# Residual stream with tokens on partitions, and its products 512 columns at a time

## The chip, the cores and the metric

The kernel runs on one core of a Trainium2 chip. The metric is the device time of one execution in microseconds (us); three runs of the kernel before are compared by their median.

## What is computed

A decoder trunk of two layers over 256 tokens of 2048 features, all in float32. The reference, cut to its frame:

```python
for layer in range(DEPTH):                       # DEPTH = 2
    if layer < N_A:                              # layer 0
        h = h + mlstm_mixer(rms_norm(h, a_norm[layer]), ...)
    else:                                        # layer 1
        k_sh, v_sh = shared_kv(h, kv_norm, w_kv, positions)
        h = h + diff_attention(rms_norm(h, b_norm[j]), k_sh, v_sh, ...)
    h = h + conv_ffn(rms_norm(h, f_norm[layer]), w_up[layer], conv_w[layer], conv_b[layer], w_down[layer])
return rms_norm(h, final_norm)
```

The mixer projects the normed stream to q and k (1024 columns each), v and an output gate o (2048 each) and 16 gate columns, runs a gated linear attention of 8 heads, multiplies by sigmoid(o) and projects with `w_out` (2048 x 2048). The attention has `w_q` (2048 columns), `w_kv` (2048 for k, 2048 for v) and `w_o`. The feed-forward has `w_up` (2048 x 11264), a convolution over three tokens, a gate, and `w_down` (5632 x 2048).

## The kernel before

**Products of halves.** Each float32 operand is split into two halves that TensorE multiplies at full rate (type fp32r): h is the rounded value, l what is left. A product is wh xh + wh xl + wl xh. The activations' halves lie side by side in one block, `xh | xl`, of 128 features by 256 tokens each.

**`gemm` (L374)** takes 256 columns of a weight matrix at a time, a "pair" of 128 columns each, and walks over the k-tiles of 128 rows. `granule` (L353) brings weights: a DMA on SyncE's queue loads 8 k-tiles (1 MB) into one of five `raw` buffers, and four k-tiles at a time ScalarE (ACT) copies the h half (L369) and VectorE (DVE) subtracts the l half (L371) into one of five `w` buffers. In the usual, "wide" form two matmuls serve a k-tile and 128 columns: the stationary wh against the 512 moving columns `xh | xl`, and wl against the 256 of xh (L411). The two halves of the PSUM bank are added up at the end: ACT copies one out (L417) and DVE adds it (L418). Pairs listed in `narrow` use three matmuls of 256 moving columns, without that addition. With `tokens_out` the activations are stationary and the weights move; the form is the same. `gemm_by_tokens` (L422) does the last 256 columns of all, the first 128 tokens ahead of the others.

In what follows a unit is one k-tile times 128 stationary columns times 256 moving ones, in its three partial products: two matmuls wide, three narrow.

**The residual stream** (`hT`, 16 tiles of 128 features by 256 tokens) has features on partitions, as the products' operands do. `residual` (L441) adds a product to it; a `Norm` (L188) then makes the next operands from the same tile (`operand`, L207: one ACT and one DVE instruction) and sums squares over features on GpSimd (POOL, L204). `rstd` (L232) gets the row sums with tiny matmuls (`sums`, L250) and spreads 1/sqrt over the partitions.

**Beginning and end.** `x` comes in two k-tiles at a time between weight loads of two k-tiles and 256 columns (`x_in`, L455), is transposed by TensorE into `x_ps` (L464), and feeds the first pair of q; the q pairs follow one another, with the 16 gate columns (`gps`, L492) among them. At the end the last product's columns are scaled, transposed back to tokens on partitions (`out_ps`, L863; `rest_ps`, L871), and scaled by the norm in `tokens_done` (L878), which writes four DMAs of 512 columns for each half of the tokens.

**What sets the order.** The code emits small work "later", a number of granules behind a product (`later`, `tick`), and the framework's scheduler then reorders the instructions of each engine by a simulated timeline. Each engine runs its list in order. Weights, `x` and the output go through SyncE's one queue.

Of the kernel before, what the change touches and what calls it, by code (L numbers as in the profile page):

```python
# [19 lines left out]
P = 128  # L20
D = 2048
# [15 lines left out]
KC = 8  # L37
HC = 4
RAW = 5
FIRST = [0, 2, 4, 6, 8, 10, 12, 14]  # L40
HL = 5
WARM = 28
HT_DVE = (0, 1, 2, 4, 6)
CW = 256

# 500000 ** (-i / 16) in float32, once for each half of a rotary pair
# [19 lines left out]
def trunk(  # L66
# [11 lines left out]
    big = ctx.enter_context(tc.tile_pool(name="big", bufs=38))  # L78
# [17 lines left out]
    waiting, clock, splits, loads = [], [0, 0], [], []  # L96
# [11 lines left out]
    # the tensor engine's clock rises with use: have it up when the first operands come  # L108
# [14 lines left out]
    # mask_a: row q, column k, NEG where k > q; mask_s: row s, column t, NEG where s > t; each twice  # L123
# [10 lines left out]
    def columns(sources, name):  # L134
        """rows of 128 parameters each, transposed: column j has parameters 128 j .. 128 j + 127"""
# [40 lines left out]
    def parameters():  # L176
# [3 lines left out]
        # w_hnorm / 2: the sigmoid of the output gate is (1 + tanh) / 2  # L180
# [4 lines left out]
    stream = resid.tile([P, KD, T], F32, name="stream")  # L185
    hT = [stream[:, i] for i in range(KD)]

    class Norm:  # L188
        """Sum of squares over the features, and the operands (h * gain) split in two exact halves."""

        def __init__(self, gain_cols, name):
            self.cols, self.name = gain_cols, name
            self.r = self.rt = self.parts = None
            self.sets = [[None] * KD for _ in gain_cols]
            self.acc = work.tile([P, T], F32, tag="acc", name=f"acc_{name}")
            self.n = 0

        def squares(self, i):
            if self.n == 0:
                act.activation(self.acc, hT[i], AF.Square)  # L200
            else:
                sq = tmp("sq")
                act.activation(sq, hT[i], AF.Square)
                pool.tensor_tensor(self.acc, self.acc, sq, op=ALU.add)  # L204
            self.n += 1

        def operand(self, n, i):  # L207
            cols, at = self.cols[n]
            g = cols[:, at + i:at + i + 1]
            h, l, hl = block(F32R, f"x_{self.name}_{i}")  # L210
            act.activation(h, hT[i], AF.Identity, scale=g)
            dve.scalar_tensor_tensor(l, hT[i], g, h.bitcast(F32), op0=ALU.mult, op1=ALU.subtract)
            self.sets[n][i] = (h, l, hl)

        def add(self, i):
            self.operand(0, i)
            self.squares(i)

        def first(self, i, ps):
            """the same from the transposed input"""  # L220
            cols, at = self.cols[0]
            g = cols[:, at + i:at + i + 1]
            h, l, hl = block(F32R, f"x_{self.name}_{i}")
            act.activation(h, ps, AF.Identity, scale=g)
            dve.scalar_tensor_tensor(l, ps, g, h.bitcast(F32), op0=ALU.mult, op1=ALU.subtract)
            self.sets[0][i] = (h, l, hl)
            if i % 8 in HT_DVE:
                dve.tensor_copy(hT[i], ps)
            else:
                act.activation(hT[i], ps, AF.Copy)  # L230

        def rstd(self):  # L232
            """1 / sqrt(mean square + eps): rt per token on partitions, a column for each half of the tokens; r on every partition"""
            with tc.high_priority():
                v = work.tile([P, 2], F32, tag="v2", name="v2")
                if self.parts is None:
                    dve.tensor_scalar(v, sums(self.acc)[:, :2], 1.0 / D, EPS, op0=ALU.mult, op1=ALU.add)
                else:
                    dve.tensor_tensor(v, self.parts[:, 0], self.parts[:, 1], op=ALU.add)
                    dve.tensor_scalar(v, v, 1.0 / D, EPS, op0=ALU.mult, op1=ALU.add)  # L240
                self.rt = rsqrt(v, "rt", dve if self.parts is None else pool)
            self.spread() if self.parts is not None else later(1, self.spread)
# [7 lines left out]
    def sums(a):  # L250
        """the sums of a over the partitions: (P, 2), tokens on partitions, a column for each half of them"""
        ps = small_ps("sum_ps")
        for t in range(2):
            pe.matmul(ps[:, t:t + 1], a[:, t * P:(t + 1) * P], ones[:, 0:1], start=True, stop=True)
        return ps
# [20 lines left out]
    def spread(y):  # L276
        """(P, 2) with tokens on partitions to (P, T) with the same T tokens on every partition"""
# [39 lines left out]
    def weighted(v, p):  # L317
        """sum over s of p[s, t] v[s, :], a bank with t on partitions for each half of t"""
# [11 lines left out]
    def squares(banks):  # L330
        """the sum of squares of a head's 256 features, (P, 2)"""
# [5 lines left out]
    def normed_rows(banks, y):  # L337
        rows = []
        for t, ps in enumerate(banks):
            rows.append(tmp("nrm"))  # L340
# [3 lines left out]
    def turn(rows, name):  # L344
        """two (128 t, 256) to features on partitions, (2, T)"""
# [7 lines left out]
    def granule(w, c0, k0, kn, raws, j, hc=None, first=False, own=True):  # L353
        """the two halves of up to HC k-tiles of 256 columns; a load brings KC of them, at the very beginning HC"""
        at, hc = k0 % KC, hc or min(HC, kn - k0)
        if at == 0:
            raws[j] = wpool.tile([P, KC, CW], F32, tag="raw", name="raw", bufs=RAW)
        part = raws[j][:, at:at + hc]
        if first or at == 0:
            n = hc if first else min(KC, kn - k0)  # L360
            loads.append(nc.sync.dma_start(raws[j][:, at:at + n], w[k0 * P:(k0 + n) * P, c0:c0 + CW].rearrange("(k p) n -> p k n", p=P)))  # L361
        if not own:
# [4 lines left out]
            return pairs, None  # L367
# [566 lines left out]
```

## Time and profile before

| what | value |
|---|---|
| median of 3 runs | 2281.06 us (2280.37 to 2281.28) |
| profiled execution, first to last instruction | 2280.0 us |
| PE busy | 2267.8 us (99%) |
| DVE, ACT, POOL busy | 70%, 55%, 8% |
| HBM read | 413.86 MB, 182 GB/s over the span |

The profiled execution has one time, its span of 2280.0 us; the median of the timed runs is 1.1 us more, so differences are made against the span and added to the median. Times of a row are microseconds from the span's start, means are ns. A matmul's end is modelled in this profile, so the busy time of one (393 ns for 512 columns) is longer than its share of a steady stream; how many start in a stretch says what one costs.

### The profile page before, as it was taken

To read this page: it belongs to the slowest core of one execution; us is meant where nothing else is said; L and a number is where in the kernel's file an instruction comes from. 1 tells how busy PE (TensorE), PEld (TensorE's weight loads), DVE (VectorE), ACT (ScalarE), POOL (GpSimd) and SP (SyncE) were. 2 spreads that over 40 slices of the span, in tenths; PEclk is the share of its full clock that TensorE was granted. 3 is DMA by queue.
4 is the path that set the end of the run, shared out by engine and by line. 5 is a ranking of instruction groups with operands and counts; after the bars stand their busy time and mean duration, and the time that the engine had idled before them with its cause. 6 is when DMAs were issued, how large, how long until landed. Compare 5 with 4: busy or idle time off the path is not lost.

```text
span 2280.0 us, 34236 instructions
## 1 busy us (share of the span) xinstructions
PE 2267.8 (99%) x13318; PEld 1995.3 (88%) x13318; DVE 1588.7 (70%) x2667; ACT 1258.4 (55%) x2019; POOL 175.7 (8%) x379
## 2 busy tenths in 40 slices
PE   9999999999999999999999999999999999999998
PEld 8888888888888888888988888988888888888887
DVE  7756667777764677775588875677777556777755
ACT  6466555655554455655554556556555445555544
POOL 2023001000000000000122213210000000000000
PEclk9999999999999999999999999999999999999999
DMA  9654566555556655565656555555555565555552
GB/s 281 186 151 150 181 187 193 185 194 188 185 178 192 202 187 185 188 190 175 200 184 191 167 159 162 179 185 185 188 192 185 171 198 192 189 191 192 174 184 89
DMA packets 415783, 418.18 MB, mean 183 GB/s; under 512 B 9134, under 2 KB 415620, under 8 KB 415620
## 3 DMA queue, kind: packets, MB, share of 16 engines
q1 hardware_dynamic: 415620, 415.98, 57.6%
q8 instruction: 105, 1.72, 0.3%
q14 instruction: 58, 0.48, 0.1%
HBM read 413.86 MB, written 2.10 MB: 182 GB/s over the span
## 4 chain that ended last, share of the span: by engine, by line
PE 99%; DMA 1%; SPq 0%; DVE 0%; ACT 0%; issue 0%; DVEq 0%; ACTq 0%
PE acc L411 95%; PE val_ps L326 1%; PE acc L435 1%; DMA raw<-in_m_w_in_dram 0%; PE as_ps L759 0%; DMA x_raw<-in_x_dram 0%; PE w_ps L572 0%; PE gps L492 0%; PE as_ps L760 0%; PE hn_ps L350 0%; PE an_ps L350 0%; PE s_ps L579 0%; PE out_ps L863 0%; PE t_ps L781 0%; SPq L361 0%; SPq L460 0%
## 5 line engine op out<-in xcount | busy, mean ns | idle before, releaser
L371 DVE TENSOR_TENSOR w<-raw,w 128x1024 fp32r<-128x1024 f32 (+1 forms) x799 | 957.9, 1199 | 563.4 <-ACT w L369 560.5
L369 ACT ACTIVATE w<-raw 128x1024 fp32r<-128x1024 f32 (+1 forms) x803 | 833.1, 1038 | 759.8 <-PE acc L411 717.2
L411 PE MATMUL acc<-x_f,w 128*128 128x512 f32 (+1 forms) x5632 | 985.1, 337 | 0.0
L411 PEld LDWEIGHTS acc<-x_f,w 128*128 128x128 f32 x5632 | 861.0, 188 | 122.0
L411 PE MATMUL acc<-hid,w 128*128 128x512 f32 (+1 forms) x2772 | 481.5, 335 | 0.0
L411 PEld LDWEIGHTS acc<-hid,w 128*128 128x128 f32 x2772 | 420.4, 188 | 57.8
L417 ACT ACTIVATE low<-acc 128x256 f32<-128x256 f32 x354 | 129.6, 384 | 188.6 <-PE acc L411 188.3
L418 DVE TENSOR_TENSOR acc<-acc,low 128x256 f32<-128x256 f32 x354 | 138.4, 430 | 71.1 <-ACT low L417 71.1
L411 PE MATMUL acc<-x_a,w 128*128 128x256 f32 (+1 forms) x1056 | 186.0, 335 | 1.3 <-ACT w L369 0.7
L411 PE MATMUL acc<-x_at,w 128*128 128x512 f32 (+1 forms) x1024 | 181.5, 338 | 0.0
L411 PEld LDWEIGHTS acc<-x_a,w 128*128 128x128 f32 x1056 | 160.2, 190 | 22.9 <-DVE w L371 1.0
L411 PEld LDWEIGHTS acc<-x_at,w 128*128 128x128 f32 x1024 | 156.7, 188 | 21.9
L658 ACT ACTIVATE c<-u,conv 128x256 f32<-128x256 f32 x176 | 95.7, 592 | 0.0
L411 PE MATMUL acc<-w,x_a 128*128 128x512 f32 (+1 forms) x512 | 93.4, 340 | 0.0
L411 PE MATMUL acc<-w,x_at 128*128 128x256 f32 (+1 forms) x544 | 93.1, 329 | 0.0
L411 PE MATMUL acc<-ao,w 128*128 128x512 f32 (+1 forms) x576 | 91.0, 319 | 0.0
L411 PE MATMUL acc<-mo,w 128*128 128x256 f32 (+1 forms) x544 | 90.3, 327 | 0.0
L411 PEld LDWEIGHTS acc<-ao,w 128*128 128x128 f32 x576 | 81.7, 188 | 8.6
L411 PEld LDWEIGHTS acc<-mo,w 128*128 128x128 f32 x544 | 80.0, 188 | 9.8
L411 PEld LDWEIGHTS acc<-w,x_at 128*128 128x128 f32 x544 | 80.3, 188 | 9.2
L411 PEld LDWEIGHTS acc<-w,x_a 128*128 128x128 f32 x512 | 78.4, 188 | 10.7
L659 DVE SCALAR_TENSOR_TENSOR c<-u,conv,c 128x255 f32<-128x255 f32 x176 | 76.9, 478 | 0.0
(255 smaller groups left out, 1159.4 us busy)
## 6 DMA issues: line engine op xcount, KB each, us to landing
raw<-in_w_up_dram SPq DMA_DIRECT2D x176, 1024.0 KB
raw<-in_w_down_dram SPq DMA_DIRECT2D x64, 1024.0 KB
raw<-in_m_w_in_dram SPq DMA_DIRECT2D x46, 1024.0 KB
raw<-in_w_kv_dram SPq DMA_DIRECT2D x32, 1024.0 KB
raw<-in_w_down_dram SPq DMA_DIRECT2D x32, 768.0 KB
raw<-in_m_w_out_dram SPq DMA_DIRECT2D x16, 1024.0 KB
raw<-in_w_q_dram SPq DMA_DIRECT2D x16, 1024.0 KB
raw<-in_w_o_dram SPq DMA_DIRECT2D x16, 1024.0 KB
```

What stands on the lines that cost most here:

```text
L326: pe.matmul(ps[:, :vh.shape[1]], a, b, start=(s == 0 and o == 0), stop=(s == t and o == 2))
L369: splits.append(act.activation(w2[:, :hc, 0], part, AF.Copy))
L371: eng.tensor_tensor(w2[:, :hc, 1], part, w2[:, :hc, 0].bitcast(F32), op=ALU.subtract)
L411: pe.matmul(to, a, b, start=(k == 0 and o == 0), stop=(k == kn - 1 and o == len(ops) - 1))
L417: act.activation(low, p[:, T:], AF.Copy)
L418: dve.tensor_tensor(p[:, :T], p[:, :T], low, op=ALU.add)
L435: pe.matmul(ps[t], a[:, s], b, start=(k == 0 and o == 0), stop=(k == kn - 1 and o == 2))
L658: act.activation(c, u, AF.Identity, bias=cw[:, 3, f:f + 1], scale=cw[:, 2, f:f + 1])
L659: dve.scalar_tensor_tensor(c[:, 1:], u[:, :T - 1], cw[:, 1, f:f + 1], c[:, 1:], op0=ALU.mult, op1=ALU.add)
```

## The change

**Stream.** It lies with tokens on partitions (`stream`, two halves of the tokens by 2048 features). `residual` adds 512 columns of a product at a time, for each half of the tokens. `Norm.squares` sums squares in ACT's own accumulator, so POOL's additions and the `sums` matmuls are gone. The next operands, which need features on partitions, are made by TensorE transposes (`turn_ps`), four for two k-tiles, and one ACT and one DVE instruction for each k-tile out of PSUM. The attention's second set of operands comes from a copy that ACT keeps.

**Products.** Everything that yields tokens on partitions (v and o of the mixer, `w_out`, `w_down` of both layers, v of the attention, `w_o`) runs in `gemm_tokens`: 512 columns at a time, activations stationary, three matmuls of 512 moving columns for a k-tile and 128 tokens. There is no second half of a bank to add. `w_up`, `w_q` and both k products stay in the wide `gemm`. The last 512 columns of the last product are two narrow pieces of 256.

**First product.** All 1024 columns of q are computed k-tile by k-tile in eight half banks, with three matmuls of 256 for each 128 columns; then come the gate columns.

**End.** The stream needs no transposing back. The final scaling is one ACT instruction over 768 columns and two DVE instructions over 256 and 1024, and two DMAs for each half of the tokens.

Five `raw` buffers become four, `big` has 44 blocks for 38. Core of the diff:

```diff
+    stream = resid.tile([P, 2, D], F32, name="stream")
...
+        def operands(self, i):
+            ps = small_ps("turn_ps")
+            for c in range(2):
+                for t in range(2):
+                    pe.transpose(ps[:, c * T + t * P:c * T + (t + 1) * P], stream[:, t, (i + c) * P:(i + c + 1) * P], ident)
+            self.scaled(0, i, ps)
+            if len(self.cols) > 1:
+                self.kept[i] = block(F32, f"kept{i}")[2]
+                act.activation(self.kept[i], ps, AF.Copy)
...
+        def add(self, g):
+            self.squares(g)
+            for i in range(2):
+                later(1, lambda i=i: self.operands(4 * g + 2 * i))
...
+    def gemm_tokens(xs, w, col0, groups, evac, cw=G, lead=1):
+        kn, hc = len(xs), WCOLS // cw // 2
+        order, last = in_order(kn, hc, groups, lead, held=4 // hc)
+        raws, accs = {}, {}
+        for j, k0 in order:
+            if k0 == 0:
+                accs[j] = [acc_ps.tile([P, 2 * T], F32, tag="acc", name="acc")[:, :cw] for _ in range(2)]
+            ps = accs[j]
+            for i, (wh, wl) in enumerate(granule(w, col0 + j * cw, cw, k0, kn, raws, j)):
+                k = k0 + i
+                xh, xl, _ = xs[k]
+                for t in range(2):
+                    s = slice(t * P, (t + 1) * P)
+                    for o, (a, b) in enumerate(((xh, wh), (xl, wh), (xh, wl))):
+                        pe.matmul(ps[t], a[:, s], b, start=(k == 0 and o == 0), stop=(k == kn - 1 and o == 2))
+            if k0 == last:
+                evac(j, accs.pop(j))
+            tick()
...
     def residual(norm):
-        def evac(j, ps):
-            for n in range(2):
-                i = 2 * j + n
-                dve.tensor_tensor(hT[i], ps[n], hT[i], op=ALU.add)
-                if norm is not None:
-                    norm.add(i)
+        def evac(g, ps):
+            for t in range(2):
+                rows = stream[:, t, g * G:(g + 1) * G]
+                dve.tensor_tensor(rows, ps[t], rows, op=ALU.add)
+            if norm is not None:
+                norm.add(g)
...
+    def first_product(evac):
...
+        x_in(0)
+        for k in range(KD):
+            if k < 4:
+                w_in(k, 1)
+            elif k % 2 == 0:
+                w_in(k, 2)
+            if k in X_AT:
+                x_in(2 + 2 * X_AT.index(k))
+            if k % 2 == 0:
+                norm_a.operands(k)
+            part = raw[0][:, k % 2]
+            w2 = wpool.tile([P, 2, HQK], F32R, tag="w2", name="w2", bufs=HL)
+            for c in ((slice(0, 512), slice(512, HQK)) if k < 2 else (slice(0, HQK),)):
+                act.activation(w2[:, 0, c], part[:, c], AF.Copy)
+                dve.tensor_tensor(w2[:, 1, c], part[:, c], w2[:, 0, c].bitcast(F32), op=ALU.subtract)
+            xh, xl, _ = xs[k]
+            for j in range(n):
+                s = slice(j * P, (j + 1) * P)
+                for o, (a, b) in enumerate(((w2[:, 0, s], xh), (w2[:, 0, s], xl), (w2[:, 1, s], xh))):
+                    pe.matmul(ps[j], a, b, start=(k == 0 and o == 0 and j % 2 == 0), stop=(k == KD - 1 and o == 2), skip_group_check=True)
...
+        dve.scalar_tensor_tensor(rows, rows, r, gain_cols(W1, T), op0=ALU.mult, op1=ALU.mult)
+        for eng, c0, c1 in ((act, 0, 768), (dve, 768, W1)):
...
+        for c0, c1 in ((0, 768), (768, D)):
+            nc.sync.dma_start(out[0, t * P:(t + 1) * P, c0:c1], stream[:, t, c0:c1])
```

Three places show how the instructions move. In the rows the line comes first, then the instruction and its tiles; a trailing number tells one buffer of a kind from the next, and x6 means six such instructions in a row.

TensorE in the down-projection of layer 0, second half of the hidden features, before:

```order
L411 MATMUL acc<-hid_7762,w_9879 128x512
L411 MATMUL acc<-hid_7762,w_9879 128x256
L411 MATMUL acc<-hid_7762,w_9879 128x512
L411 MATMUL acc<-hid_7762,w_9879 128x256
L411 MATMUL acc<-hid_7772,w_9879 128x512
L411 MATMUL acc<-hid_7772,w_9879 128x256
```

And TensorE in the same half now, where the activations (`hid`) are the stationary operand:

```order
L413 MATMUL acc<-w_9045,hid_6928 128x512 x6
L413 MATMUL acc<-w_9045,hid_6938 128x512 x6
L413 MATMUL acc<-w_9060,hid_7138 128x512 x6
L413 MATMUL acc<-w_9060,hid_7148 128x512 x6
L413 MATMUL acc<-w_9077,hid_7348 128x512 x6
```

The alternation of 512 and 256 moving columns gives way to runs of 512 alone.

TensorE at the beginning of the q product of the attention, behind layer 0's last down-projection, before (the row sums of the norm):

```order
L411 MATMUL acc<-x_at_10537,w_11046 128x256
L411 MATMUL acc<-x_at_10537,w_11046 128x512
L411 MATMUL acc<-x_at_10537,w_11046 128x256
L254 MATMUL sum_ps<-ones,acc_at 128x1 x2
L411 MATMUL acc<-x_at_10664,w_11046 128x512
L411 MATMUL acc<-x_at_10664,w_11046 128x256
```

And now, 22 matmuls into that product:

```order
L387 MATMUL acc<-x_at_9445,w_9908 128x512
L387 MATMUL acc<-x_at_9445,w_9908 128x256
L207 MATMUL turn_ps<-ident,stream 128x128 x2
L387 MATMUL acc<-x_at_9445,w_9908 128x512
L207 MATMUL turn_ps<-ident,stream 128x128 x6
L387 MATMUL acc<-x_at_9445,w_9908 128x256
```

Eight transposes of the last 512 features stand inside the product that will need them from its 49th matmul on; the row sums are gone.

TensorE at the first product, before:

```order
L464 MATMUL x_ps<-ident,x_raw 128x128 x8
L411 MATMUL acc<-x_a_157,w_170 128x256 x6
L411 MATMUL acc<-x_a_164,w_170 128x256 x2
L464 MATMUL x_ps<-ident,x_raw 128x128 x2
L411 MATMUL acc<-x_a_164,w_170 128x256 x4
```

And now:

```order
L207 MATMUL turn_ps<-ident,stream 128x128 x8
L484 MATMUL acc<-x_a_163,w_169 128x256 x24
L484 MATMUL acc<-x_a_166,w_199 128x256 x4
L207 MATMUL turn_ps<-ident,stream 128x128 x4
L484 MATMUL acc<-x_a_166,w_199 128x256 x20
```

A k-tile feeds 24 matmuls in a row instead of six, and the first of them still stand behind eight transposes.

More of the change, by code (lines that the diff above doesn't have):

```diff
@@ L93, in small_ps @@
         return sm_ps.tile([P, 512], F32, tag="sm", name=name)
-    waiting, clock, splits, loads = [], [0, 0], [], []
+    waiting, clock, loads = [], [0, 0], []
     def later(granules, fn):
@@ L192, in __init__ @@
             self.cols, self.name = gain_cols, name
-            self.r = self.rt = self.parts = None
+            self.r = self.rt = None
+            self.kept = {}
             self.sets = [[None] * KD for _ in gain_cols]
[L195 to L205, printed above, removed]
@@ L207, in operand @@
-        def operand(self, n, i):
-            cols, at = self.cols[n]
[L209 to L230, printed above, removed]
+            self.parts = work.tile([P, 2, NG], F32, tag="parts", name=f"parts_{name}")
@@ L391, in gemm @@
             ps = accs[j]
-            if before is not None:
-                before(k0, ends[k0])
-            halves, w2 = granule(w, c0, k0, kn, raws, j, ends[k0] - k0, before is not None)
+            halves = granule(w, col0 + j * CW, CW, k0, kn, raws, j)
             wide = j not in narrow
@@ L451, in trunk @@
     norm_a = Norm([(gain_a, 0)], "a")
-    norm_a.parts = work.tile([P, 2, 2], F32, name="parts", bufs=1)
-    x_raw = [None, None]
-    def x_in(k0, k1):
-        c, at = divmod(k0, KC)
-        if at == 0:
-            x_raw[c] = wpool.tile([P, KC, CW], F32, tag="raw", name="x_raw", bufs=RAW).rearrange("p k n -> p (k n)").rearrange("p (t c) -> p t c", t=2)
-        cols = slice(at * P, (at + k1 - k0) * P)
-        nc.sync.dma_start(x_raw[c][:, :, cols], x[0, :, k0 * P:k1 * P].rearrange("(t p) c -> p t c", p=P))
-        for i in range(k1 - k0):
-            ps = small_ps("x_ps")
-            for t in range(2):
-                pe.transpose(ps[:, t * P:(t + 1) * P], x_raw[c][:, t, (at + i) * P:(at + i + 1) * P], ident)
-            norm_a.first(k0 + i, ps[:, :T])
@@ L635, in mlstm, with evac_o @@
[L635 to L636 removed]
+            hn[h] = normed_rows(banks, y, block(F32, f"hn{h}")[:2])
+        def evac_o(g, ps):
+            for c in range(2):
+                h, rows = 2 * g + c, []
+                for t in range(2):
+                    o = tmp("o")
+                    act.activation(o, ps[t][:, c * VD:(c + 1) * VD], AF.Tanh, scale=rt_half[:, t:t + 1])
+                    dve.scalar_tensor_tensor(o, o, 1.0, hn[h][t], op0=ALU.add, op1=ALU.mult)
+                    rows.append(o)
+                later(1, lambda h=h, rows=rows: turned(h, rows))
@@ L637, in mlstm, with turned @@
+        def turned(h, rows):
+            ps = turn(rows, "hn_ps")
+            for n in range(2):
+                i = 2 * h + n
+                outs[i] = scaled_split(ps[:, n * T:(n + 1) * T], half_h[:, i:i + 1], f"mo{i}")
+        rt_half = work.tile([P, 2], F32, name="rt_half", bufs=1)
+        later(10, parameters_in)
+        later(13, parameters)
+        first_product(evac_q)
+        dve.tensor_scalar(rt_half, norm.rt, 0.5, None, op0=ALU.mult)
         gates()
-        gemm(xs, w, 0, [3], evac_q)
@@ L795, in scaled @@
         def scaled(h, banks, y):
-            normal = normed_rows(banks, y)
+            normal = normed_rows(banks, y, [tmp("nrm") for _ in range(2)])
             later(1, lambda: placed(h, normal))
@@ L808, in evac_q_and_operands @@
             evac_q(j, ps)
-            norm.operand(1, 2 * j)
-            norm.operand(1, 2 * j + 1)
+            norm.second(2 * j)
         gemm(norm.sets[0], w_q[0], 0, range(8), evac_q_and_operands)
         gemm(norm.sets[1], w_kv, 0, range(8), rotated(k, "ak", softmax))
-        gemm(norm.sets[1], w_kv, AQK, range(8), evac_v, tokens_out=True, narrow=[7])
+        gemm_tokens(norm.sets[1], w_kv, AQK, range(4), evac_v)
         return outs
@@ L859, in turned @@
-    def turned(j, scaled):
-        for t in range(2):
-            ps = small_ps("out_ps")
-            for n in range(2):
-                pe.transpose(ps[:, n * P:(n + 1) * P], scaled[n][:, t * P:(t + 1) * P], ident)
-            act.activation(stream[:, 2 * j + t], ps[:, :T], AF.Copy)
-    def rest_of_stream():
-        for t in range(2):
-            ps = small_ps("rest_ps")
-            for n in range(2):
-                pe.transpose(ps[:, n * P:(n + 1) * P], hT[2 * last + n][:, t * P:(t + 1) * P], ident)
-            rest[t] = block(F32, f"rest{t}")[0]
-            act.activation(rest[t], ps[:, :T], AF.Copy)
```

259 lines of the change are left out of this document (118 added, 141 removed).

## The prediction

> **What bounds the kernel.** I read the page first: the busy times, the chain of work that ended last, and the costliest groups.
>
> ```profile
> PE 2267.8 (99%) x13318; PEld 1995.3 (88%) x13318; DVE 1588.7 (70%) x2667; ACT 1258.4 (55%) x2019; POOL 175.7 (8%) x379
> ...
> PE 99%; DMA 1%; SPq 0%; DVE 0%; ACT 0%; issue 0%; DVEq 0%; ACTq 0%
> ...
> L369 ACT ACTIVATE w<-raw 128x1024 fp32r<-128x1024 f32 (+1 forms) x803 | 833.1, 1038 | 759.8 <-PE acc L411 717.2
> L417 ACT ACTIVATE low<-acc 128x256 f32<-128x256 f32 x354 | 129.6, 384 | 188.6 <-PE acc L411 188.3
> ```
>
> TensorE is the path from end to end. ACT, which makes the weights' halves, sits idle until TensorE frees a buffer (717.2 us), never the other way. So what leaves ACT, DVE and POOL is worth nothing by itself; here that is the addition of the second halves (L417, L418) for the products with tokens out, POOL's sums, and the scaling at the end. The change is worth what TensorE's list gets shorter by, plus the first 25 us and the last 8.
>
> What a matmul costs in a steady stream I take from a stretch with nothing but wide products (busy time and, in brackets, matmuls of TensorE), and from pieces of the chain in order of time (start, length, count):
>
> ```profile
> 500.00:1100.00 600.00, 600.00 (x3439) 525.81 (x3438) 412.76 (x646) 327.23 (x483) 6.84 (x9) 1.00 0.59 188
> ```
>
> ```profile
> 47.87 3.69 PE gps L492 x16
> 51.56 27.47 PE acc L411 x157
> ...
> 163.62 5.50 PE acc L411 x31
> ...
> 1147.87 0.34 PE sum_ps L254 x4
> ...
> 1251.65 0.43 PE as_ps L759 x2
> ...
> 2248.51 0.43 PE out_ps L863 x4
> ...
> 2255.38 6.50 PE acc L435 x55
> ```
>
> A wide unit is two matmuls: 2 x 600 / 3439 = 348.9 ns. The 55 narrow matmuls of 256 columns take 118.2 ns each, a narrow unit 354.6. The gate product is the only stream of 512 columns alone, all fp32r: 3.69 / 16 = 230.6 ns, which is also what is left in a wide unit beside 118.2 (230.7). A transpose costs 0.43 / 4 = 107.5 ns.
>
> **Products with tokens out.** v, o, `w_out`, `w_o` and the attention's v have 256 units each, `w_down` 704 in layer 0 and, without its last 512 columns, 616 in layer 1: 2600 units. Before, 172 of them were narrow (the last pair of `w_out`, 32; of layer 0's `w_down`, 44; of the attention's v, 32; the first and last of `w_o`, 64) and 2428 wide: 2428 x 0.3489 + 172 x 0.3546 = 908.1 us. Now each is one and a half matmuls of 512 columns, 3900 in all: 3900 x 0.2306 = 899.3 us. The columns streamed are the same; what goes is the 256-column matmul, which costs 2.2 ns more than half of a 512. That is -8.8 us, and the 44 units in the last 512 columns that turn from wide to narrow give back 44 x 5.7 ns = 0.3: **-8.5 us**.
>
> The 230.6 is the sum's largest doubt: a nanosecond is 3.9 us. Below it the nearest row is the attention's scores (L759, two passes of a float32 matmul, 215 ns each), which would give another -61 us, but that is another number format. Above it stand the products of the mixer's v, whose 31 matmuls from 163.62 on take 177.4 ns against 174.4 in the wide stretch, 1.7% more, though a switch to and from the small matmuls is in them; 1.7% on 899.3 is +15. I keep to the gate product, the nearest in format and length.
>
> The Trainium skill ("TensorE: Matmul & The Clock Gate", section on the back-to-back issue gap) gives a warm gap of N / 2.4 + 2.5 ns, a fixed cost that does not depend on length. As an estimate from that page, 109.2 and 215.8 ns would make the wide unit 325.0, the narrow 327.6 and the new one 323.7, and the saving 3.8 us where the rows give 8.8. The rows lie above both of its figures, and the sum goes by the rows.
>
> **Transposes.** The stream's operands for three norms cost 3 x 32 transposes; the end loses 28 (`out_ps`) and 4 (`rest_ps`); x had 32 and keeps them. 64 x 0.1075 = +6.9 us, in TensorE's list and hidden by nothing. The four row sums go: 4 x 0.34 = -1.4. Together **+5.5 us**.
>
> **The last operands.** At three places (`w_out` to the first up product, layer 0's `w_down` to the attention's q, `w_o` to the second up product) a product's last 512 features are the next one's k-tiles 12 to 15. Before, they needed no transpose.
>
> ```profile
> L371 DVE TENSOR_TENSOR w<-raw,w 128x1024 fp32r<-128x1024 f32 x764 | 933.3, 1222 | 559.3 <-ACT w L369 558.3
> ...
> L445 DVE TENSOR_TENSOR stream<-acc,stream 128x256 f32<-128x256 f32 x80 | 30.1, 416 | 3.2 <-PE acc L411 3.1
> ...
> L371 DVE TENSOR_TENSOR w<-raw,w 128x512 fp32r<-128x512 f32 x35 | 24.6, 702 | 4.1 <-ACT w L369 2.2
> ...
> L225 DVE SCALAR_TENSOR_TENSOR x_a<-x_ps,gain_a,x_a 128x256 fp32r<-128x256 f32 x16 | 7.6, 477 | 1.2 <-ACT x_a L224 1.2
> ...
> L553 DVE SCALAR_TENSOR_TENSOR mq<-acc,rstd_a 128x256 f32<-128x256 f32 x6 | 2.3, 418 | 0.1
> ...
> L266 DVE TENSOR_TENSOR rs_u<-rt 128x2 f32<-128x2 f32 x9 | 1.4, 160 | 0.2
> ```
>
> DVE's list there holds two additions of 512 columns (416 plus 260 for 256 more columns, by 1222 against 702: 0.68 each), a weight split, some 15 small steps of the norm, another split, and the first operand: 1.4 + 1.2 + 2.4 + 1.2 + 0.5 = 6.7 us. TensorE reaches it after 48 matmuls and 8 transposes, 48 x 0.1744 + 0.86 = 9.2 us: 2.5 spare. The next three operands have two splits among them, 3.9 us, against 12 matmuls, 2.1: 0.7 spare. ACT and DVE wait there for the transposes with weight splits queued behind them, which five `w` buffers cover. I put 0.2 us on each place for what a semaphore adds: **+0.6 us**.
>
> **First product.** Windows of two microseconds (PE, PEld, DVE, ACT, POOL busy; granted clock; DMA share; GB/s), and the timeline:
>
> ```profile
> 4.00:6.00 2.00, 0.81 (x7) 0.55 (x5) 0.17 (x1) 0.49 (x1) 0.00 (x0) 1.00 0.93 296
> 6.00:8.00 2.00, 1.50 (x9) 1.37 (x10) 1.83 (x5) 1.92 (x6) 0.00 (x0) 0.80 0.95 309
> 8.00:10.00 2.00, 2.00 (x11) 2.00 (x11) 2.00 (x6) 1.29 (x3) 0.36 (x1) 0.50 1.06 337
> 10.00:12.00 2.00, 2.00 (x17) 2.00 (x16) 1.25 (x4) 1.04 (x4) 1.17 (x1) 0.85 1.11 364
> ```
>
> ```profile
> 5.51 0.63 ACT L369 ACTIVATE w<-raw 128x512 fp32r<-128x512 f32 x1 [3.51 <-DMA raw<-in_m_w_in_dram]
> ...
> 6.05 1.74 ACT L224 ACTIVATE x_a<-x_ps,gain_a 128x256 fp32r<-128x256 f32 x4
> 6.17 0.69 DVE L371 TENSOR_TENSOR w<-raw,w 128x512 fp32r<-128x512 f32 x1 [1.74 <-ACT w L369]
> ...
> 6.50 0.63 PE L464 MATMUL x_ps<-ident,x_raw 128*128 128x128 f32 x4 [1.69 <-DMA x_raw<-in_x_dram]
> ...
> 6.88 2.08 PE L411 MATMUL acc<-x_a,w 128*128 128x256 f32 x8
> ```
>
> Before, the first matmul starts at 6.88. Now x (256 KB) and 512 KB of weights come first, the bytes that had landed at 6.50. ACT then splits twice (0.63) before the operand (0.47, x_a being 1.74 for four with other work between): first matmul at 8.2. DVE, two splits of 0.69 behind ACT and then the l half of the operand (0.48), releases the second one at 9.0. The clock is halved from about 7.2 to 10.6 (0.80, 0.50 and 0.85 in the windows), so the 1.6 us to 10.6 do half their work: 0.8 lost. Then 384 x 0.1182 = 45.4, 24 transposes 2.6, the norm's spreading and a parameter transpose 0.6, the gates 3.7: 9.0 + 0.8 + 45.4 + 2.6 + 0.6 + 3.7 = 62.1. Before, gates and q are done 64 matmuls into the piece at 51.56: 51.56 + 64 x 0.1744 = 62.7. **-0.6 us**, between -2 and +2. DMA doesn't bind: a k-tile brings 640 KB in 24 x 0.118 = 2.84 us, 231 GB/s against the 337 that moved in a window. The eight results leave by eight DVE instructions of 418 ns; the k product wants the first two banks, done 12 matmuls and two gate matmuls earlier (1.42 + 0.46 = 1.9 against 4 x 0.42 = 1.7); without that cover it costs 1.7.
>
> **End.**
>
> ```profile
> 2271.89 0.42 DVE L882 TENSOR_TENSOR rest<-acc,rest 128x256 f32<-128x256 f32 x1 [4.21 <-PE acc L435]
> ...
> 2273.93 1.31 ACT L895 ACTIVATE stream<-stream,end 128x256 f32<-128x256 f32 x3 [0.69 <-DVE end L889]
> 2273.93 1.14 DVE L897 TENSOR_SCALAR stream<-stream,end 128x256 f32<-128x256 f32 x4
> 2274.99 0.48 DVE L893 SCALAR_TENSOR_TENSOR stream<-rest,end,gain_rows 128x256 f32<-128x256 f32 x1
> ```
>
> The chain to the factor r (2273.93) stays. The first output DMA could leave after one ACT instruction of three; now it waits for 768 columns in one, between 0.9 and 1.3 us, and the same megabyte follows: +0.3 to +0.8, less what fewer, longer rows save. I take **+0.4 us**.
>
> **Sum.** -8.5 + 5.5 + 0.6 - 0.6 + 0.4 = -2.6 us against the span of 2280.0; on the median of 2281.06 that is 2278.4. About 0.2% (4.6 us: 2276.5 to 2285.6) is what a measurement of this kernel can tell from no change, so the forecast is no difference, on the fast side.
>
> **Rivals.**
>
> *512 columns stream cheaper.* The gate product is a sample of 16, its first matmul among them. At 229.0 ns in place of 230.6 the products give 6.2 us more: 2272.2. It decides from 230.1 on, half a nanosecond below my row. For it: a run of 512 alone has no 256-column matmul with its dearer share. Against: the share of the 512 in a wide unit agrees with my row to 0.1 ns.
>
> *A second stretch of half clock.* The first stretch came after 4 to 6 us, when TensorE was busy for 0.81 of 2 us. Now it transposes and waits until 9.0; if that counts as idle, the clock stays down for another 3.4 us, half of it lost: +1.7, 2280.1. The Trainium skill (the same page, sections on the clock gate and on PE-mode transpose) has windows of about 3.4 us whose activity sets the clock, and says that transposes don't count as busy. The length agrees with the 7.2 to 10.6 here.
>
> *The last operands come late.* If at the three places the two splits have to be waited for (2 x 1.22) and the last operand behind them (0.48), each costs 2.9: +8.8, 2287.2, slower. It decides from 2.4 us a place on. For it: 0.7 us spare is thin, and DVE's list is fixed. Against: a split can run as soon as its buffer is free, and before, TensorE had no idle time ahead of this product:
>
> ```profile
> L411 PE MATMUL acc<-x_at,w 128*128 128x512 f32 (+1 forms) x1024 | 181.5, 338 | 0.0
> ```
>
> *512 columns dearer.* With the mixer's 1.7% the products give 14.9 less: 2293.3, slower.
>
> **Chances.** The forecast 0.38 and the second half-clock stretch 0.09 (both within 0.2%: 0.47), the cheaper stream 0.38 (faster), the late operands 0.10 and the dearer stream 0.05 (slower: 0.15). The likeliest time is 2278.4. The range goes from 2269.5 (228.3 ns a matmul) to 2287.5 (late operands), and leaves out the dearer stream and the ends of the others. The forecast's own range is 2276.5 to 2285.6.
>
> **What would show it.** In the changed profile: 3900 matmuls of 512 columns at 230.6 ns from start to start; 128 `turn_ps` transposes at 107.5; the gates and the first product done by 62 us; no idle TensorE before the k-tiles 12 of the three products; the last matmul 8 us before the end. The forecast is wrong if a stream of 512 alone runs below 230 or above 232.5 ns, if the three places show microseconds of waiting, or if the first product starves for weights.

## The result, and the profile after

The changed kernel takes 2288.12 us (median of 6 runs, 2286.86 to 2288.88) against 2280.94 for the kernel before on the same chip: ratio 1.0031, 95% interval 1.0020 to 1.0043. It is 7.2 us slower where the forecast said 2.6 faster. The profiled execution spans 2286.8 us, 6.75 more than that of before. The page's busy times and chain:

```profile
PE 2272.3 (99%) x12034; PEld 1937.2 (85%) x12034; DVE 1516.2 (66%) x2445; ACT 1209.0 (53%) x1840; POOL 111.2 (5%) x305
...
PE 98%; DMA 1%; SPq 0%; DVE 0%; ACT 0%; issue 0%; DVEq 0%; ACTq 0%
...
L352 ACT ACTIVATE w<-raw 128x1024 fp32r<-128x1024 f32 x768 | 813.3, 1059 | 790.3 <-PE acc L413 396.1
```

The bound is the same: TensorE, with ACT waiting for it. TensorE has 1284 matmuls fewer and is busy 4.5 us longer. The chain's DMA reads 1% in both kernels, but 1% is some 20 us. In order of time, the chain's head (start, length, what) in the kernel before is

```profile
5.22 5.92 DMA x_raw<-in_x_dram
...
11.15 10.50 DMA raw<-in_m_w_in_dram
...
21.73 1.07 ACT w L369
...
24.11 14.72 PE acc L411 x85
```

and in the changed kernel

```profile
6.80 9.87 DMA stream<-in_x_dram
16.73 8.07 DMA raw<-in_m_w_in_dram
26.74 6.04 DMA raw<-in_m_w_in_dram
32.87 1.06 ACT w L478
...
35.70 18.41 PE acc L484 x140
```

TensorE takes the chain over at 24.11 before and at 35.70 now. Until then the loads, and the splits that wait for them, set the end in both kernels. The forecast counted TensorE's work from 9.0 us on.

Why the load issued at 26.74 is so late stands in SyncE's timeline (start, length; the `rows` and `gate_b` loads bring parameters):

```profile
16.73 0.40 SPq L463 DMA_DIRECT2D raw<-in_m_w_in_dram  x1
19.31 0.31 SPq L172 DMA_DIRECT2D rows<-in_kv_norm_dram  x1
...
24.82 0.23 SPq L172 DMA_DIRECT2D rows<-in_lam_q_dram  x1
...
26.35 0.29 SPq L175 DMA_DIRECT2D gate_b<-in_m_b_fgate_dram  x1
26.74 1.41 SPq L463 DMA_DIRECT2D raw<-in_m_w_in_dram  x3
```

Thirteen small loads stand between the weights of k-tiles 8 and 9 (16.73) and those of 10 to 15 (26.74), and some wait for earlier transfers: the one at 24.82 starts just after the weights issued at 16.73 have landed (16.73 + 8.07 = 24.80). In the windows (busy times as in the prediction's; then granted clock, DMA share, GB/s) DMA stands all but still from 24 to 28 us, and TensorE pays later:

```profile
24.00:26.00 2.00, 2.00 (x19) 2.00 (x19) 1.37 (x9) 1.09 (x2) 0.00 (x0) 1.00 0.03 9
26.00:28.00 2.00, 2.00 (x19) 2.00 (x18) 2.00 (x3) 0.92 (x1) 0.00 (x0) 1.00 0.23 23
32.00:34.00 2.00, 0.66 (x6) 0.46 (x5) 0.04 (x1) 1.13 (x2) 0.00 (x0) 1.00 1.05 422
...
38.00:40.00 2.00, 2.00 (x12) 2.00 (x11) 1.90 (x3) 0.74 (x3) 0.00 (x0) 0.54 0.17 22
```

TensorE stalls although it doesn't need those weights yet. ACT's list has the split of k-tile 10's weights (the `w` at 32.87, which waits 3.73 us) ahead of the operand of k-tile 7 (one of the two `x_a` at 33.83):

```profile
32.87 1.06 ACT L478 ACTIVATE w<-raw 128x1024 fp32r<-128x1024 f32 x1 [3.73 <-DMA raw<-in_m_w_in_dram]
33.83 0.82 ACT L282 ACTIVATE x_a<-turn_ps,gain_a 128x256 fp32r<-128x256 f32 x2
```

After the stall the granted clock is halved until about 39.8 (0.54 in the last window above). From start to start the wait is 2.6 us, and 3.4 us at half clock lose 1.7.

The rest of the kernel is compared by stages, from start to start. TensorE's rows for layer 0's first down product, second up product (1408 matmuls, code not changed) and second down product are, before,

```profile
648.48 123.59 PE L411 MATMUL acc<-hid,w 128*128 128x512 f32 x704
771.92 245.42 PE L411 MATMUL acc<-x_f,w 128*128 128x512 f32 x1408
1017.18 123.69 PE L411 MATMUL acc<-hid,w 128*128 128x512 f32 x748
```

and after

```profile
656.20 122.68 PE L413 MATMUL acc<-w,hid 128*128 128x512 f32 x528
778.72 246.57 PE L387 MATMUL acc<-x_f,w 128*128 128x512 f32 x1408
1025.12 35.74 PE L413 MATMUL acc<-w,hid 128*128 128x512 f32 x153
...
L413 PE MATMUL acc<-w,hid 128*128 128x512 f32 (+1 forms) x2112 | 477.7, 388 | 0.0
...
L207 PE MATMUL turn_ps<-ident,stream 128*128 128x128 f32 x128 | 19.3, 278 | 3.0 <-DMA stream<-in_x_dram 3.0
```

The down product goes from 123.44 to 122.52 us: 232.05 ns for each of 528 matmuls of 512 columns, not 230.6, and 348.1 ns for a unit against 350.7. The up product, whose 1408 matmuls stand in the same order and wait for nothing in either kernel, goes from 245.26 to 246.40. TensorE nowhere waits ahead of `gemm_tokens` (0.0 idle), and the only wait ahead of a transpose is for x at the start.

### The profile page after: what moved, and what is told of

Same layout as the page of the kernel before. It is cut to its first block, busy times and chain, and to the rows that moved or that the text cites. A ratio compares the mean times of both kernels' runs of the same rounds, so it can differ in the third digit from the quotient of the medians.

```text
span 2286.8 us, 31046 instructions
## 1 busy us (share of the span) xinstructions
PE 2272.3 (99%) x12034; PEld 1937.2 (85%) x12034; DVE 1516.2 (66%) x2445; ACT 1209.0 (53%) x1840; POOL 111.2 (5%) x305
## 4 chain that ended last, share of the span: by engine, by line
PE 98%; DMA 1%; SPq 0%; DVE 0%; ACT 0%; issue 0%; DVEq 0%; ACTq 0%
PE acc L387 53%; PE acc L413 40%; PE acc L484 1%; PE val_ps L311 1%; PE acc L431 1%; DMA raw<-in_m_w_in_dram 1%; PE turn_ps L207 0%; DMA stream<-in_x_dram 0%; PE as_ps L768 0%; PE w_ps L593 0%; PE gps L510 0%; PE as_ps L769 0%; PE an_ps L333 0%; PE hn_ps L333 0%; PE s_ps L600 0%; SPq L463 0%
## 5 line engine op out<-in xcount | busy, mean ns | idle before, releaser
L353 DVE TENSOR_TENSOR w<-raw,w 128x1024 fp32r<-128x1024 f32 x768 | 938.6, 1222 | 620.6 <-ACT w L352 619.4
L352 ACT ACTIVATE w<-raw 128x1024 fp32r<-128x1024 f32 x768 | 813.3, 1059 | 790.3 <-PE acc L413 396.1
L413 PE MATMUL acc<-w,hid 128*128 128x512 f32 (+1 forms) x2112 | 477.7, 388 | 0.0
L413 PEld LDWEIGHTS acc<-w,hid 128*128 128x128 f32 x2112 | 387.3, 188 | 87.5
L413 PE MATMUL acc<-w,x_a 128*128 128x512 f32 x768 | 183.3, 396 | 0.0
L387 PE MATMUL acc<-x_at,w 128*128 128x256 f32 (+1 forms) x1024 | 181.9, 338 | 0.0
L413 PE MATMUL acc<-w,ao 128*128 128x512 f32 x384 | 92.2, 397 | 0.0
L413 PE MATMUL acc<-w,x_at 128*128 128x512 f32 x384 | 91.9, 396 | 0.0
L413 PE MATMUL acc<-w,mo 128*128 128x512 f32 x384 | 91.3, 397 | 0.0
L669 DVE SCALAR_TENSOR_TENSOR c<-u,conv,c 128x254 f32<-128x254 f32 x176 | 76.8, 477 | 0.1
```

Of the source, the lines that this page charges most:

```text
L352: act.activation(w2[:, :hc, 0], part, AF.Copy)
L353: dve.tensor_tensor(w2[:, :hc, 1], part, w2[:, :hc, 0].bitcast(F32), op=ALU.subtract)
L387: pe.matmul(to, a, b, start=(k == 0 and o == 0), stop=(k == kn - 1 and o == len(ops) - 1))
L413: pe.matmul(ps[t], a[:, s], b, start=(k == 0 and o == 0), stop=(k == kn - 1 and o == 2))
L669: dve.scalar_tensor_tensor(c[:, 2:], u[:, :T - 2], cw[:, 0, f:f + 1], c[:, 2:], op0=ALU.mult, op1=ALU.add)
```

## The experiments

Each ran beside the kernel before, whose median was 2280.8 to 2280.9 throughout.

**Parameters behind the weights.**

```diff
-        later(10, parameters_in)
-        later(13, parameters)
+        later(15, parameters_in)
+        later(16, parameters)
```

> The changed kernel with the small parameter loads issued behind the last weight load of the first product instead of behind that of k-tiles 8 and 9. Theory (the start): the weights of k-tile 10 are late because twelve small loads stand ahead of them on SP's queue, ACT's list has their split ahead of the operand of k-tile 7, and TensorE first waits 2.6 us at 32 to 36 us and then runs at half clock until 39.8, 1.7 us more. Both go: 4.3 us less than the changed kernel, 2283.8, with no gap of TensorE over 0.3 us after its first product has begun, and no granted clock below 1.0 after 13 us. Rival (the first product takes 640 KB for each k-tile and DMA itself doesn't keep up): the wait only moves to another k-tile, under 1 us less.

2284.02 us, 4.1 less than the changed kernel where 4.3 were expected (ratio to before 1.0013, 1.0004 to 1.0022). The chain now passes to TensorE at 7.95 and stays there through the first product:

```profile
7.95 1.12 PE turn_ps L207 x4
9.06 5.51 PE acc L484 x28
...
15.01 3.31 PE acc L484 x28
...
18.43 10.36 PE acc L484 x88
...
30.43 5.07 PE acc L484 x44
```

So the late weights are shown, and with them more than half of the 7.2 us. One part of the expectation missed: the first 28 matmuls take 5.51 us, 197 ns each against 118 for the next 28, so a half clock after the start is still there, though the granted clock of this profile reads 1.00. The same window of this run and of the changed kernel, whose profile has the half clock:

```profile
10.00:12.00 2.00, 2.00 (x11) 2.00 (x11) 1.95 (x4) 2.00 (x5) 0.00 (x0) 1.00 1.06 411
10.00:12.00 2.00, 2.00 (x11) 2.00 (x11) 1.57 (x3) 2.00 (x5) 0.00 (x0) 0.50 1.05 408
```

**Warming matmuls in the idle time.** Placed behind x's first four transposes:

```diff
+            if self.name == "a" and i == 0:
+                with tc.issue_after(turned.ins):
+                    for _ in range(48):
+                        pe.matmul(warm_ps[:, :P], warm, warm, start=True, stop=True)
```

> The changed kernel with 48 more warming matmuls (128 columns, bf16) on TensorE behind the transposes of x's first two k-tiles, where it stands idle from 5.5 to 8.5 us; the transposes of k-tiles 2 and 3 thereby move behind the first four matmuls. Theory: the half clock from 9.1 to 12.5 us comes from the idle time before, and goes: 1.7 us less, and 0.3 to 0.5 for the earlier first matmul, 2 us less in all, 2286.0. Rival (the half clock comes however TensorE was used before, or from what DMA and the other engines take): at most 0.5 us less, with the granted clock still 0.5 in a window after 9 us.

The mechanism came true and the time didn't: 2289.09 us, 1.0 more than the changed kernel. Windows at the start and at the stall:

```profile
10.00:12.00 2.00, 2.00 (x20) 2.00 (x19) 1.69 (x3) 2.00 (x5) 0.00 (x0) 1.00 1.05 406
...
28.00:32.00 4.00, 3.47 (x29) 3.14 (x26) 1.02 (x4) 0.00 (x0) 0.00 (x0) 1.00 0.83 248
32.00:36.00 4.00, 1.44 (x6) 1.15 (x7) 2.15 (x6) 1.82 (x4) 0.00 (x0) 0.81 1.02 417
```

20 matmuls run between 10 and 12 us (11 in the changed kernel): the half clock of the start is gone. TensorE then stands 3.1 us in 28 to 36, and the same weights release it. The Trainium skill ("TensorE: Matmul & The Clock Gate", section on why this matters for your kernels) says to leave no gap over about 3 us between bursts of matmuls. For the start the clock here agrees: behind a wait of 3.0 us it was halved, and with the wait filled it wasn't. But behind the changed kernel's stall, two waits of 1.7 and 0.6 us with four matmuls between them, it was halved as well, so here less waiting than the Trainium skill's 3 us was enough. The end of the product didn't depend on the half clock of the start.

**Both edits.**

> Both edits of the start together: the small parameter loads behind the first product's weights, and the 48 warming matmuls. Alone the first gave 4.1 us, the second nothing, and its trace shows the granted clock at 1.00 from 8 to 16 us but TensorE waiting 4.0 us in place of 2.5 for the same late weights. Theory (the half clock after the start does cost its 2 us, and the wait for the weights had swallowed the gain): 2 us less than with the loads alone, 2282.0. Rival (the first product is bound by its loads from the start on): the same 2284.0 as with the loads alone, with a new wait of 2 us before 35 us.

2282.93 us, 1.1 less than with the loads alone (ratio to before 1.0010, 1.0001 to 1.0019): little more than half of the 2.0 expected. In the chain a load stands again, until 25.19, and TensorE has it from 29.27 on:

```profile
17.56 7.63 DMA raw<-in_m_w_in_dram
...
29.27 4.88 PE acc L488 x40
```

**The same warming in the kernel before** (24 matmuls behind its first four transposes).

> The kernel before with 24 more warming matmuls on TensorE behind its first four transposes, where it stands idle from 4.8 to 6.5 us. Theory (idle time there brings the half clock from 7.2 to 10.6 us, as in the changed kernel): it goes, 1.7 us less than before, 2279.2. Rival (the first product waits for x and weights anyway, or the warming matmuls push its first transposes back): within 0.5 us of before.

2280.87 us, as before (ratio 0.9999, 0.9990 to 1.0007). The half clock goes there too, and two windows show where the gain went (the busy time of TensorE stood at 4.00 and 2.83 of 4 us without the warming):

```profile
8.00:10.00 2.00, 2.00 (x19) 2.00 (x19) 1.86 (x5) 1.56 (x5) 0.28 (x1) 1.00 1.00 330
16.00:20.00 4.00, 3.41 (x29) 3.17 (x28) 2.44 (x8) 3.18 (x8) 2.40 (x2) 1.00 1.11 330
20.00:24.00 4.00, 3.15 (x23) 2.52 (x22) 2.58 (x6) 2.93 (x5) 0.18 (x1) 1.00 1.07 334
```

The kernel before never paid for its half clock; its loads did not come faster.

**An earlier first matmul.** On top of both edits: the first weights in two loads, x's second tile behind the second k-tile's weights, operands ahead of splits, later transposes behind the first 12 matmuls, and 24 warming matmuls.

```diff
-X_AT = (0, 2, 3, 5, 6, 8, 9)
+X_AT = (1, 2, 3, 5, 6, 8, 9)
...
+                for c0 in (0, 512):
+                    loads.append(nc.sync.dma_start(raw[0][:, 0, c0:c0 + 512], w[:P, c0:c0 + 512]))
```

> The changed kernel with both edits of the start (24 warming matmuls here), and its first weights in two loads of 512 columns, x's second tile behind the second k-tile's weights, the first operands ahead of the weights' splits on ACT, and the transposes of later k-tiles behind the first 12 matmuls. Theory: the first matmul starts at 6.9 us or earlier in place of 8.3, and the first product ends 1.5 us earlier than with both edits alone (2282.9): 2281.4, still 0.5 above the kernel before. Rival (the weights' loads bind from there on): the gain comes back as waits before 30 us, under 0.5 us.

2285.21 us, 2.3 worse than both edits alone. The first matmul starts at 8.08, not 6.9, and an operand of k-tile 4 is late:

```profile
8.08 2.23 PE L500 MATMUL acc<-x_a,w 128*128 128x256 f32 x16 [1.22 <-ACT w L494]
...
23.34 22.45 PE L500 MATMUL acc<-x_a,w 128*128 128x256 f32 x188 [0.75 <-DVE x_a L290]
```

The start explains only a part. Between the two profiles the k product's first matmul moves from 61.88 to 62.58, 0.7 us, and layer 1's two up products, whose code is the same, go from 247.41 to 247.85 and from 246.11 to 246.55. Why they do wasn't tested.

**Without the transposes of the three norms.** The operands are scaled from the stream's rows as they lie.

```diff
-            ps = small_ps("turn_ps")
...
+            else:
+                ps = stream[:, 0, i // 4 * G:(i // 4 + 1) * G]
```

> The changed kernel without the 96 transposes of the stream for the norms f0, at and f1: the operands are scaled and split straight from the stream's rows, so that part of the computation is left out (the operands lie untransposed). Theory (transposes cost their list time and nothing else): 96 x 0.1086 = 10.4 us less than the changed kernel, 2277.7. Rival (the operands come late at the product boundaries, or the transposes' banks hold up others): 13 us less or more. Second rival (transposes overlap other streams): 7 us less or under.

2277.62 us, 10.5 less than the changed kernel: 109 ns for each of 96, the forecast's 107.5 within the runs' spread. They cost their time in TensorE's list; the 13 us and the 7 us of the two rivals are out.

**512 columns by themselves.** The first parts of both `w_down` use the halves of their first two k-tiles over and over, the second part of layer 0 splits one load over and over. Only stages are read from this run, which was one execution.

> The changed kernel with three down products cut: the first parts of both layers use the halves of their first two weight granules over and over (no loads, no splits), the second part of layer 0 splits one load over and over (splits, no loads); most of the weights are left out there. What is read is the time of 528 matmuls of 512 columns in each of these stages, 122.5 us in the changed kernel (232.0 ns each). Theory A (a stream of 512 columns costs 232 ns in itself): 122.5 us in all of them, within 0.3. Theory B (230.6 ns in itself, the rest is what ACT and DVE do in SBUF beside it): 121.8 us without splits and loads, and 122.5 with the splits alone. Theory C (the rest comes from the weights' DMA): 121.8 in both.

The rows of layer 0's first down product and of what follows:

```profile
654.14 122.68 PE L424 MATMUL acc<-w,hid 128*128 128x512 f32 x528
776.66 246.57 PE L387 MATMUL acc<-x_f,w 128*128 128x512 f32 x1408
```

122.52 us again, without a load or a split beside it from 660 us on (theory A); the stage with splits alone takes 125.44 us up to the next product and layer 1's 122.65, as in the changed kernel. The 232 ns is no cost of the other engines. The Trainium skill ("SBUF — State Buffer", section on who interferes with whom) says that TensorE never waits on another's accesses there; this run agrees.

**The matmuls of the products undone.** 256 columns at a time, one matmul of 512 and one of 256 in 2336 of 2600 units; the residual and its transposes stay.

```diff
+                    for o, (a, b, to) in enumerate(((xh, w2[:, i].rearrange("p a n -> p (a n)"), ps[t]), (xl, wh, ps[t][:, :T]))):
+                        pe.matmul(to, a[:, s], b, start=(k == 0 and o == 0), stop=(k == kn - 1 and o == 1))
```

> The changed kernel with the matmuls of its tokens-out products undone: 256 columns of weights at a time, one matmul of 512 (first halves against both halves of the weights) and one of 256 for each unit, in 2336 of 2600 units (the last three groups of 512 in layer 1's second w_down part stay). All else, the residual with tokens on partitions and its transposes among it, stays. Theory (the new products do save, 348.4 ns for a unit against the 350.6 that the kernel before shows in its w_down stages): 2336 x 2.2 = 5 us more than the changed kernel, 2293.3. Rival 1 (the forecast's prices, 348.9 against 345.9, hold, and the time is lost elsewhere): 7 us more. Rival 2 (streams of 512 alone save nothing): within 1 us of the changed kernel.

2292.24 us, 4.1 more than the changed kernel. Layer 0's first down product shows 349.9 ns for a unit ((779.64 - 656.49) / 352), 1.8 above the changed kernel's 348.1, and 2336 x 1.8 = 4.2, near the 4.1. That they meet is in part chance: in this profile the k product starts at 65.88 for 67.14, and all that stands behind it takes 4.8 us more, near the 5 expected.

```profile
656.49 123.31 PE L434 MATMUL acc<-w,hid 128*128 128x512 f32 x704
779.64 246.45 PE L387 MATMUL acc<-x_f,w 128*128 128x512 f32 x1408
```

The new products do save, by less than the 7 us that the forecast's prices would give (rival 1).

**What sets a matmul's price.** These runs leave the products and their order as they are. The first adds three warming matmuls at the start, the others move only where tiles lie, or nothing.

```diff
-WARM = 28
+WARM = 31
```

> The changed kernel with 31 warming matmuls for 28, so that every later instruction of TensorE lies three matmuls further on in its program; nothing else. Up products whose code is the same in both kernels take 245.26 and 246.25 us before, 246.40 and 246.11 changed, to 0.02 us in each of four variants, so something fixed sets the price of a matmul there. Theory A (the place of the instructions in TensorE's program): the stages move by 0.3 us or more each, up or down. Theory B (the place of the operands in SBUF): they stay within 0.03 us.

No stage behind the start moved by more than 0.02 us (time 2288.77, as the changed kernel): moving the matmuls on by three places in TensorE's program changed nothing.

```diff
-        b = big.tile([P, 2 * T + 4], dt, tag="block", name=name)
+        b = big.tile([P, 2 * T + 8], dt, tag="block", name=name)
```

> The changed kernel with blocks of 520 columns for 516, so that the operands lie at other places in SBUF; the list of each engine is the same. Theory A (the place of the instructions sets a matmul's price): each stage within 0.03 us of the changed kernel. Theory B (the place of the operands): the stages move by 0.3 us or more each.

The same, 2288.30, but the run says nothing: as the next expectation tells, blocks are padded to the same 2080 bytes either way, so nothing had moved. The next run did move them (2T + 12 columns).

> The changed kernel with blocks of 524 columns and 43 of them, for 516 and 44: now the operands do lie at other places (2112 bytes apart; the run with 520 columns had moved nothing, because blocks are padded to 2080 bytes either way). The list of each engine is the same. Theory B (the place of the operands in SBUF sets a matmul's price): the stages move by 0.3 us or more each against the changed kernel (layer 0's second up product 246.40 us, layer 1's 246.11, layer 0's first down product 122.52). Rival: within 0.03 us, and the price comes from something else.

2286.82 us, 1.3 less. Stages moved by 0.1 to 0.6 us either way, the last down product's 512 columns from 107.71 to 107.09, the attention's q and k from 191.25 to 191.70. Of the stages named in the expectation all moved by 0.14 to 0.28 us: less than the 0.3 that theory B asked for, more than the rival's 0.03.

> The kernel before, profiled a second time. If its prices are as fixed as those of the changed kernel, its up products of layer 0 (second part) and layer 1 (second part) take 245.26 and 246.25 us again, and its down products of the first parts 123.44 and 123.52, each within 0.03. If one execution differs from the next, they move by some tenths, and the difference of 1.1 us to the changed kernel in layer 0 says nothing.

245.26, 246.25, 123.43 and 123.52 us, in a second profile of the kernel before: behind the first product, stages repeat to 0.01 us from one execution to the next. The first product doesn't; the mixer's v starts at 107.4 us here and at 108.8 in the first profile.

```diff
-    big = ctx.enter_context(tc.tile_pool(name="big", bufs=44))
-    wpool = ctx.enter_context(tc.tile_pool(name="wpool", bufs=3))
+    wpool = ctx.enter_context(tc.tile_pool(name="wpool", bufs=3))
+    big = ctx.enter_context(tc.tile_pool(name="big", bufs=44))
```

> The changed kernel with its two pools, blocks and weights, allocated in the other order, so that all of the operands lie at other places in SBUF; the list of each engine is the same. Theory (the place sets a matmul's price, and made the up products of layer 0 dearer by 1.1 us each): stages move by up to 1 us and the whole by up to 2 us, either way. Rival (place matters by tenths only, as in the run with blocks of 524 columns, and the 1.1 us come from something else): no up product moves by more than 0.3 us.

> The kernel before with its two pools allocated in the other order; the list of each engine is the same. Theory: its up products of layer 0, the cheapest of all here (245.26 us), move by up to 1 us, and its whole time by up to 2 us; if 245.26 was a lucky place, it rises. Rival: no stage moves by more than 0.3 us, and the whole stays within 0.5 us.

The changed kernel falls to 2286.02 us, 2.1 less; the kernel before rises to 2284.04, 3.1 more (ratio 1.0014, 1.0005 to 1.0023), both by more than the 2 us expected. Layer 0's second up product and the start of what follows, in the changed kernel with its pools swapped,

```profile
778.19 245.09 PE L387 MATMUL acc<-x_f,w 128*128 128x512 f32 x1408
1023.12 35.73 PE L413 MATMUL acc<-w,hid 128*128 128x512 f32 x153
```

and in the kernel before with its pools swapped:

```profile
771.97 247.13 PE L411 MATMUL acc<-x_f,w 128*128 128x512 f32 x1408
1018.93 123.19 PE L411 MATMUL acc<-hid,w 128*128 128x512 f32 x748
```

244.93 us for 246.40, and 246.96 for 245.26: the two kernels change places. The order of each engine's instructions is the same, and only the operands' places in SBUF differ, so these places move the price of a matmul, here by up to 0.7 per cent.

**Start and places together.**

> The changed kernel with both edits of the start and blocks of 524 columns. If the two add up, 2282.9 less 1.3, 2281.6, still 0.7 over the kernel before; if the places' gain was the start's chance, 2282.9.

2281.57 us: they add up. That is 6.6 less than the changed kernel and not to be told from the kernel before (ratio 1.0004, 0.9995 to 1.0013). No version that computes the whole beats the kernel before.

## Why the prediction was wrong

Its terms against what the profiles and runs give, in us:

| term | forecast | measured | from |
|---|---|---|---|
| first product | -0.6 | +4.6 | k product's first matmul at 67.14 against 62.58 |
| tokens-out products | -8.5 | -5.4 | what the other rows leave of 6.75 |
| up products (not changed) | 0 | +2.0 | twice 1.14 in layer 0, twice -0.14 in layer 1 |
| transposes less row sums | +5.5 | +5.6 | 64 x 0.109 - 1.4 |
| last operands | +0.6 | 0 | no idle time ahead of them |
| end | +0.4 | 0 | 8.40 us behind the last matmul against 8.43 |
| sum | -2.6 | +6.75 | |

The first row compares two executions: in the second profile of the kernel before the k product starts at 61.19, which would make it +5.9. The third row is no gain or loss of the change, as said below. Without these two the rest is -5.4 + 5.6, next to nothing: what the transposes cost is what the products save.

**The step that failed first** is "DMA doesn't bind". It compared a k-tile's 640 KB with a rate that DMA can move, and the rate was there (422 GB/s at 32 to 34 us). It didn't ask when the loads are issued. The prediction named 24 transposes and 384 matmuls, but not SyncE's list, where the parameter loads now stand ahead of six k-tiles' weights, nor ACT's, where a split that waits for them stands ahead of an operand that doesn't. Moving the loads gave back 4.1 us. Its last condition, that the first product might starve for weights, was what happened, and had been given no chance.

It also charged 0.8 us for the half clock and took both kernels' first products to be bound by TensorE. In the kernel before, loads have the chain until 21.65 us, so neither its half clock nor its first matmul's start set the end: taking the half clock away there gave nothing.

**The second** is the mis-sized term: 230.6 ns for a matmul of 512 columns came from 16 matmuls of the gate product. In the new products it is 232.05 to 232.8, between the row taken and the 1.7% that stood as a rival. The saving was partly kept by luck: the wide units of these stages had also cost more, 350.7 where the window of 600 us gave 348.9. The direction was right: undoing the matmuls alone costs 4.1 us.

**The third** had no term at all. Code that wasn't changed was priced at nothing, and layer 0's up products became dearer by 2.3 us. That place alone can do this is shown, 1.5 and 1.7 us on this very stage. That it did so between these two kernels is argued, not shown: the order and the waits of that stage are the same in both. Which addresses matter, and why, stays open. It is luck of the layout either way: with the pools of both kernels swapped they lie 2.0 us apart in place of 7.2.

**What held**: the price of the transposes, the last operands on time at the three boundaries, the end, and the absence of any new bound behind the first product. The rival of late operands reached the measured time almost to the microsecond, by a mechanism that is nowhere in the trace. The rival of a second half clock came true as a row (36 to 40 us) and as a consequence of the stall, not of the start. In another execution of the same start it came true as it was meant: the profile of the 512 columns by themselves has the half clock from 7.4 to 14.2 us,

```profile
12.00:14.00 2.00, 2.00 (x11) 2.00 (x11) 1.90 (x3) 0.85 (x2) 0.00 (x0) 0.50 1.04 424
```

and the k product starts there at 65.08, before the 67.14 of the changed kernel's profile: TensorE comes to the stall later, waits 0.8 us in 32 to 36 in place of 2.3, and the clock stays whole behind it. Two small numbers of the prediction have no row: the 0.2 us a place for a semaphore, where no waiting was found, and the 2.2 ns between a 256-column matmul and half of a 512, which its own prices make 2.9; no sum uses that one.

## What to carry to other kernels

Read the chain in order of time, not only its shares: "DMA 1%" of 2 ms is the whole start, and there the order in which a queue issues its loads, and what stands behind a waiting instruction in an in-order list, decide, not the rate. Before trusting a difference of 0.2% between two builds, build each a second time with its operands elsewhere: here that alone moved one kernel by 3.1 us up and the other by 2.1 down, together 5.2 of the 7.2 us between them. A stream's price to half a per cent is to be taken from a stage of hundreds of matmuls, and even then it belongs to one layout.

## What the hardware showed that I had not expected

- A matmul's price depends on where its operands lie, and repeats: 1408 matmuls took 245.26 and 246.96 us in two layouts of one program, and 245.26 again in another execution.
- Neither loads nor splits beside it changed the stream: 122.52 us for 528 matmuls with both and with neither.
- A half clock cost nothing where loads set the pace: without it the kernel before took 2280.87 us, as with it.
- A profile's granted clock can miss a half clock: it read 1.00 over 28 matmuls that took 197 ns each.
- A half clock at the start lasted 3.4 us in one execution and 6.8 in another, with the same instructions up to there.
